# A hybrid decoder layer: the gates of the third and the last recurrent head move behind the last head's levels and scores

## The chip, the cores and the metric

The kernel runs on one core of a Trainium2 chip. The metric is the device time of one execution in microseconds (us). A core has a matrix engine (TensorE, PE in the profile), a vector engine (VectorE, DVE), a scalar engine (ScalarE, ACT), GpSimd (POOL) and a sync engine (SyncE, SP), which issues the transfers here. Each runs its own queue of instructions in order and waits for the others by semaphores.

## The reference

One decoder layer on 2048 tokens of width 1024, in float32. An RMS norm is followed by one projection whose columns feed two groups of heads. Their outputs, side by side, go through an output projection and are added to the input; a gated MLP with a causal depthwise convolution of width 3 and a last RMS norm follow.

The first group has four recurrent heads (HGRN2) of key and value width 128:

```python
f = lb + (1.0 - lb) * jax.nn.sigmoid(hf)
# S_t = diag(f_t) S_{t-1} + k_t v_t^T,  o_t = S_t^T q_t  (k_t = 1 - f_t)
o_hg = hgrn2_chunkwise(q_hg, 1 - f, v_hg, log(f))
o_hg = rmsnorm(o_hg, hg_norm_w) * silu(hg)
```

The last factor is the head's gate: `silu(g) = g * sigmoid(g)`, with g a projection of the normed input. The second group is attention with a window of 128 keys: eight query heads on two key heads, with a learned sink logit in each softmax.

## The kernel before

The sequence is worked in two halves of 1024 tokens, one after the other. In each half the loop of the stage called "mix" runs over h = 0 to 3. Step h holds one recurrent head and one pair of attention heads (attention j = h). After the four steps come the output projection (`out_proj`), the gate and up projections of the MLP (`gate_up`) and the down projection (`down`). Texts count the heads from 1: the third head is h = 2, the last is h = 3.

Activations stand with features on the 128 partitions and tokens along the free axis. To keep float32 accuracy with fast matmuls, an operand is split in two parts, hi and lo (`split`, lines 208 and 209, and for weights `prep`, lines 178 and 179: a cast on ACT and a subtraction on DVE), and three products are added. A projection, `unit` (line 197), is 8 x 3 x 2 = 48 matmuls of 128x512 into two PSUM banks. The banks come in three sets: "mm" with four, "hg" and "at" with two each.

A recurrent head (`hgrn`) is a Python generator that hands back control at its `yield`s:

- f and q: two projections ("f" and "hq" in the profile), a sigmoid, and q into one of eight slots named "hg".
- levels: K = 1 - f and Q = q f (line 433; both have one buffer), the diagonal products (`pdiag`, line 441), then for m = 1, 2, 4, 8, 16, 32, 64 a set of products `plev` (lines 467 and 480) between neighbouring blocks of m tokens, each followed on DVE by an update of K and Q (lines 473, 474, 483, 484) and by a masked copy into ST. The next level's products need the updated K (gathered by ACT into G, line 465) and Q. F, the running product of f, starts as the f tile itself.
- state: K is transposed (`pkn`), the chunk updates `pu` are formed, and a chain of eight DVE steps makes the states SS.
- gate: the projection g (`gate`), its product with the norm factors `invb` (line 450, into q's tile, since q has been used up), sigmoid (line 451), product (line 452).
- output: 16 products `po` (lines 531 and 532), squares on ACT (line 533), an inverse root on DVE, scaling to `on`, transposes `pot` back (line 545), and the product of `pot`, the norm weight and the gate (line 546) into mix[h].

For the last head, the gate comes before the levels, and mix[3] is split at once (lines 550 and 551).

Attention (`attend`) has four parts: the projection of q ("q", slot "att"), scores with softmax (`psc`, then `sc`, lines 343 to 383), and for each group of 512 tokens the transposes `ppt` and products with V (`poT`). `project_v` makes the recurrent values for two heads at a time, at h = 0 and h = 2.

`out_proj` needs mix[0] to mix[7] in split form. The split tiles take the places of the half's input X, which become free only when the last projection of the stage has read them. Each of its units goes over the eight inputs in the order 0, 4, 1, 5, 2, 6, 7, 3, so a unit can begin before mix[7] and mix[3] exist. Its second unit may start only behind the last head's level m = 8, its third only behind `po` (`AFTER`).

The order in which each engine gets its instructions isn't the program's order alone. The program is handed to a scheduler, which plays it through with its own model of durations: among the instructions that could go, the one that stands earlier in the program goes first. So an early place is a priority, and a projection that stands late can still be taken as filling where nothing earlier is ready. Tiles of one tag share a fixed number of buffers: "f" (the f tile, the gate's sigmoid) has two, K, Q and SS one.

The loop over the heads calls the generators by `next`:

```python
next(hg); next(hg); next(at)        # f and q, levels, attention q
# values at even h, weights of the gate
next(at); next(hg); next(hg)        # scores, state, gate
next(at); next(at); next(hg)        # two groups of V products, output
```

Step 3 goes in another order: f and q, attention q, gate, six splits, levels, scores, state, first group of V, output, second group.

Of the kernel before, what the change touches and what calls it, by code (L numbers as in the profile page):

```python
# [8 lines left out]
F32 = mybir.dt.float32  # L9
# [3 lines left out]
AF = mybir.ActivationFunctionType  # L13
ALU = mybir.AluOpType
# [3 lines left out]
P = 128  # L18
# [3 lines left out]
HALF = 1024  # L22
# [3 lines left out]
HG = 4  # L26
# [19 lines left out]
def hymba_layer(ctx: ExitStack, tc: tile.TileContext, a: dict, out: bass.AP):  # L46
    nc = tc.nc
# [22 lines left out]
    def halves():  # L70
        return [(b, slice(b * 512, (b + 1) * 512)) for b in range(NB)]
# [132 lines left out]
    def split(src, w=None, eng=None, dst=None):  # L204

        h, l = dst or new_x()
        if w is None:
            nc.scalar.copy(h, src)
            (eng or nc.vector).tensor_tensor(l, src, h.bitcast(F32), op=ALU.subtract)  # L209
        else:  # L210
            nc.scalar.activation(h, src, AF.Identity, scale=w)
            nc.vector.scalar_tensor_tensor(l, src, w, h.bitcast(F32), op0=ALU.mult, op1=ALU.subtract)
        return h, l
# [68 lines left out]
    def blocks(t, turn=False):  # L282

        v = t.rearrange("p (g r) -> p g r", r=32)
        return v[:, :, ::-1] if turn else v
# [131 lines left out]
    def hgrn(hf, h, X, invb, vs, WG, mix, p, fu=None):  # L417

        fu = fu or unit(a["w_f"][h], X, "f")
        f = p.tile([P, HALF], F32, tag="f", name="f", bufs=2)  # L420
# [4 lines left out]
        q = slot(f"hg{h}")  # L425
# [17 lines left out]
                                    ident.unsqueeze(1).to_broadcast([P, 4, P]), op=ALU.mult)  # L443


        def gate():
            gu = unit(WG.get(h, a["w_g"][h]), X, "g")
            s = p.tile([P, HALF], F32, tag="f", name="sg", bufs=2)
            for b, bs in halves():
                nc.vector.tensor_tensor(blocks(q[:, bs], b), blocks(gu[b]), blocks(invb[:, bs]), op=ALU.mult)  # L450
                nc.scalar.activation(s[:, bs], q[:, bs], AF.Sigmoid)
                nc.vector.tensor_tensor(q[:, bs], q[:, bs], s[:, bs], op=ALU.mult)

        if h == HG - 1:
            gate()
            yield
        F = f
        for m in LEVELS:
            nb = HALF // (2 * m)
# [35 lines left out]
            for s0 in range(0, P, 2 * m):  # L495
                nc.scalar.copy(ST[s0:s0 + m, :, s0 + m:s0 + 2 * m],
                               pl[s0:s0 + m, 0:TT * m].rearrange("p (c m) -> p c m", c=TT))
        yield
        v = vs[h]

        Kn = p.tile([P, TT, P], F32, tag="t4", name="Kn", bufs=2)
# [7 lines left out]
        for b in range(NB):  # L509
# [4 lines left out]
            for i in range(4):  # L514
# [3 lines left out]
                                               op0=ALU.mult, op1=ALU.add)  # L518
        yield
        g = q  # L520
        if h < HG - 1:
            gate()
            yield
        on = p.tile([P, TT, P], F32, tag="t4", name="on", bufs=2)
# [9 lines left out]
        rs = rsqrt(ss, TT, 1.0 / P)  # L534
# [7 lines left out]
        for b, bs in halves():  # L542
            pt = ps("hg", "pot")
            for i in range(4):
                nc.tensor.transpose(pt[:, i * P:(i + 1) * P], on[:, 4 * b + i], ident)
            nc.vector.scalar_tensor_tensor(blocks(g[:, bs]), blocks(pt, b), C.hgw, blocks(g[:, bs]),
                                           op0=ALU.mult, op1=ALU.mult)
            if h == HG - 1:
                hi, lo = mix[h]
                nc.scalar.copy(hi[:, bs], g[:, bs])  # L550
                nc.vector.tensor_tensor(lo[:, bs], g[:, bs], hi[:, bs].bitcast(F32), op=ALU.subtract)
        nc.vector.tensor_copy(state[:, h], SS[:, TT - 1])
        yield

    def project_v(hf, pr, X, rs, p):

# [416 lines left out]
    X, W = [], []  # L973
# [5 lines left out]
    f0 = unit(a["w_f"][0], X, "f", kind="aux", then={4: xs.spread})  # L979
    nxt = X, kv, xs.acc, xs.rs, f0  # L980
    for hf in range(NH):
        X, kv, invb, rs, f0 = nxt
        with ExitStack() as st:
            p = pool(f"mix{hf}", stack=st, reuse_waits="tile")
            KS, V = att_keys(hf, kv, invb, p)
            mix = [None] * KT
            vs = []
            M, WG = {}, {}
            for h in range(HG):
                hg = hgrn(hf, h, X, invb, vs, WG, mix, p, f0 if h == 0 else None)  # L990
                at = attend(hf, h, X, invb, KS, V, mix, p)
                next(hg)
                if h == HG - 1:
                    next(at)
                    next(hg)
                    for kt in (0, 4, 1, 5, 2, 6):
                        M[kt] = split(mix[kt])
                    next(hg)
                else:
                    next(hg)  # L1000
                    next(at)
                if h % 2 == 0:
                    vs += project_v(hf, h // 2, X, rs, p)
                if h < HG - 1:
                    WG[h] = prep(a["w_g"][h])
                next(at)
                next(hg)
                if h < HG - 1:
                    next(hg)
                next(at)  # L1010
                if h < HG - 1:
                    next(at)
                    next(hg)
                else:
                    next(hg)
                    next(at)
            M[7], M[3] = mix[7], mix[3]
        with ExitStack() as st:
            p = pool(f"ffn{hf}", stack=st, reuse_waits="tile")
            kept, ops, hs, first = out_proj(hf, M, p)  # L1020
            acts = gate_up(hf, ops, hs, first, p)
            nxt = down(hf, kept, acts, p)
# [62 lines left out]
```

## Time and profile before

| what | us |
|---|---|
| time before, median of 3 runs | 2219.83 (2214.84 to 2221.45) |
| the profiled execution's own time | 2216.09 |
| its span, first to last instruction | 2214.4 |
| PE busy | 2173.3 |
| DVE busy | 1637.8 |
| ACT busy | 1047.8 |
| first matmul of the output projection, first half | 336.3 |
| first matmul of gate_up, first half | 462.8 |
| first matmul of down, first half | 880.7 |

A profile comes from one execution. Lines such as L197 are lines of the kernel, `out<-in` names the tile written and the tiles read. A float32 matmul of two unsplit operands is listed as two matmuls. Matmuls are pipelined, so their listed durations overlap.

### The profile page before, as it was taken

Reading aid. Unit: us, or ns where it says so; the run is one execution under the profiler, and the core shown is the slowest. Engines: PE = TensorE matmul, PEld = TensorE weight load, DVE = VectorE, ACT = ScalarE, POOL = GpSimd, SP = SyncE. Lnnn points to the kernel's source line nnn. Section 1 sums busy time; section 2 is a strip of 40 time slices with the busy share of each in tenths; the row PEclk is TensorE's granted clock in tenths of the full one; section 3 lists DMA queues with packets and bytes.
Section 4 is the critical chain, followed back from the end, with each engine's and each line's share of the span. In section 5 each row is a group of like instructions: output and inputs, shape, how many; then the busy total and the mean of one; then the engine's idle time right before and its main releaser. Section 6 shows DMA issues by size and latency. Waiting matters only on the chain.

```text
span 2214.4 us, 29214 instructions
## 1 busy us (share of the span) xinstructions
PE 2173.3 (98%) x11302; PEld 1818.8 (82%) x11302; DVE 1637.8 (74%) x2458; ACT 1047.8 (47%) x1821; POOL 13.0 (1%) x37
## 2 busy tenths in 40 slices
PE   8999998999999999999999999989999999999997
PEld 6988987778888888888889889878788888888887
DVE  6567568688887888775865666577878888887766
ACT  6445445454444445335725455545544444443353
POOL 2000000000000000000000000000000000000000
PEclk9999999999999999999999999999999999999998
DMA  4111112322333234964631111213232323359643
GB/s 154 39 29 39 29 39 67 107 84 92 113 100 114 88 127 146 372 233 160 201 124 39 29 29 39 67 29 132 66 126 85 124 87 119 96 196 388 223 130 128
DMA packets 89995, 254.15 MB, mean 115 GB/s; under 512 B 11008, under 2 KB 13184, under 8 KB 89856
## 3 DMA queue, kind: packets, MB, share of 16 engines
q1 hardware_dynamic: 87552, 251.17, 33.8%
q8 instruction: 88, 1.44, 0.3%
q10 hardware_dynamic: 2304, 1.12, 0.2%
q14 instruction: 51, 0.42, 0.1%
HBM read 195.10 MB, written 57.15 MB: 114 GB/s over the span
## 4 chain that ended last, share of the span: by engine, by line
PE 94%; DVE 3%; ACT 1%; DMA 1%; issue 0%; SPq 0%; DVEq 0%; ACTq 0%
PE X L697 7%; PE X L698 7%; PE X L699 7%; PE pop L197 6%; PE hq L197 4%; PE f L197 4%; PE q L197 4%; PE g L197 4%; PE pdx L879 4%; PE pdx L880 4%; PE pdx L881 4%; PE Y L697 4%; PE Y L699 4%; PE Y L698 4%; PE pdy L880 3%; PE pdy L879 3%
## 5 line engine op out<-in xcount | busy, mean ns | idle before, releaser
L574 ACT CAST whi<-raw 128x1024 fp32r<-128x1024 f32 x88 | 92.7, 1053 | 109.3 <-PE X L698 66.8
L698 PE MATMUL X<-T,whi 128*128 128x512 f32 x352 | 137.3, 390 | 0.0
L697 PE MATMUL X<-T,whi 128*128 128x512 f32 x352 | 137.0, 389 | 0.0
L699 PE MATMUL X<-T,wlo 128*128 128x512 f32 x352 | 136.9, 389 | 0.0
L763 DVE SCALAR_TENSOR_TENSOR y<-ga,cw,y 128x1024 f32<-128x1024 f32 x88 | 112.5, 1279 | 28.1 <-ACT y L761 28.1
L703 ACT COPY u<-X 128x512 f32<-128x512 f32 x88 | 51.6, 587 | 121.6 <-PE X L699 121.3
L575 DVE TENSOR_TENSOR wlo<-raw,whi 128x1024 fp32r<-128x1024 f32 x88 | 107.2, 1218 | 0.0
L575 DVE TENSOR_TENSOR xld<-raw,xhd 128x1024 fp32r<-128x1024 f32 x72 | 80.8, 1132 | 18.9 <-ACT xhd L574 18.6
L178 ACT CAST whi<-raw 128x1024 fp32r<-128x1024 f32 (+2 forms) x61 | 63.0, 1035 | 62.0 <-PE hq L197 12.4
L574 ACT CAST xhd<-raw 128x1024 fp32r<-128x1024 f32 x72 | 69.6, 978 | 43.2 <-DMA raw<-act0T 14.7
L197 PE MATMUL pop<-XL,whi 128*128 128x512 f32 x256 | 84.8, 395 | 3.5 <-DVE XL L209 3.5
L197 PE MATMUL pop<-XH,wlo 128*128 128x512 f32 x256 | 83.8, 393 | 0.8 <-DVE wlo L179 0.8
L197 PE MATMUL pop<-XH,whi 128*128 128x512 f32 x256 | 84.1, 400 | 0.2
L179 DVE TENSOR_TENSOR wlo<-raw,whi 128x1024 fp32r<-128x1024 f32 (+2 forms) x61 | 73.2, 1204 | 13.2 <-ACT whi L178 13.2
L697 PEld LDWEIGHTS X<-T,whi 128*128 128x128 f32 x352 | 66.1, 188 | 14.0 <-ACT u L703 0.3
L699 PEld LDWEIGHTS X<-T,wlo 128*128 128x128 f32 x352 | 66.1, 188 | 13.9 <-issue 0.2
L698 PEld LDWEIGHTS X<-T,whi 128*128 128x128 f32 x352 | 66.1, 188 | 13.9 <-issue 0.2
L879 PE MATMUL pdx<-xhd,hid 128*128 128x512 f32 x192 | 74.5, 391 | 1.0 <-ACT hid L574 1.0
L880 PE MATMUL pdx<-xld,hid 128*128 128x512 f32 x192 | 74.8, 390 | 0.0
L697 PE MATMUL X<-T,Sh 128*128 128x512 f32 x176 | 68.7, 390 | 5.3 <-ACT s L703 5.3
L881 PE MATMUL pdx<-xhd,lod 128*128 128x512 f32 x192 | 73.7, 389 | 0.0
L567 PE MATMUL pvv<-whi,XL 128*128 128x256 f32 x256 | 73.1, 287 | 0.0
(359 smaller groups left out, 6530.8 us busy)
## 6 DMA issues: line engine op xcount, KB each, us to landing
wr<-in_w_down SPq DMA_DIRECT2D x90, 512.0 KB, 5.6
raw<-in_w_gate SPq DMA_DIRECT2D x44, 512.0 KB, 3.7
raw<-in_w_up SPq DMA_DIRECT2D x44, 512.0 KB, 3.6
raw<-act0T SPq DMA_DIRECT2D x20, 512.0 KB, 5.9
raw<-act1T SPq DMA_DIRECT2D x20, 512.0 KB, 5.6
act0B<-y SPq DMA_DIRECT2D x33, 256.0 KB, 2.3
act1B<-y SPq DMA_DIRECT2D x33, 256.0 KB, 2.5
raw<-in_w_out SPq DMA_DIRECT2D x16, 512.0 KB, 4.0
```

What stands on the lines that cost most here:

```text
L179: nc.vector.tensor_tensor(lo[:, c], raw[:, c], hi[:, c].bitcast(F32), op=ALU.subtract)
L197: nc.tensor.matmul(o[b], w, x[:, bs], start=f, stop=l)
L567: nc.tensor.matmul(o[:, 0:256], xl[:, t], hi[:, c], start=False, stop=False)
L574: nc.scalar.copy(h, src)
L575: (eng or nc.vector).tensor_tensor(l, src, h.bitcast(F32), op=ALU.subtract)
L697: nc.tensor.matmul(o, wh[:, ws], xh, start=i == 0 and not more, stop=False, skip_group_check=more)
L698: nc.tensor.matmul(o, wh[:, ws], xl, start=False, stop=False, skip_group_check=more)
L699: nc.tensor.matmul(o, wl[:, ws], xh, start=False, stop=i == 3, skip_group_check=more)
L763: nc.vector.scalar_tensor_tensor(y, g[:, w:w + HALF], C.cw[:, ft, w:w + 1], y, op0=ALU.mult, op1=ALU.add)
L879: nc.tensor.matmul(o, wh[:, i, c], ah[:, i, cols], start=f, stop=False, skip_group_check=more)
L880: nc.tensor.matmul(o, wh[:, i, c], al[:, i, cols], start=False, stop=False, skip_group_check=more)
L881: nc.tensor.matmul(o, wl[:, i, c], ah[:, i, cols], start=False, stop=l, skip_group_check=more)
```

## The change

The loop handles heads 1 and 2 as before. Heads 3 and 4 are written out with the generators of both open at once:

- third head: f and q, levels, attention q, values, scores, state; then f and q of the last head; then the third head's first group of V, its output without the gate, its second group of V;
- last head: attention q, levels, scores;
- the gate of the third head, the gate of the last head, the six splits;
- the last head's state, first group of V, output, second group of V.

For the third head (`late`) the output is evicted from PSUM by ACT with the norm weight as scale into q's tile. Its gate, which comes later, puts g times `invb` in a tile of its own ("ug", tag "f"), and has one product more: q by ug, then q by the sigmoid. The third head's gate weights are no longer loaded ahead at an explicit place but inside its projection.

```diff
+        late = h == HG - 2
+
         def gate():
             gu = unit(WG.get(h, a["w_g"][h]), X, "g")
             s = p.tile([P, HALF], F32, tag="f", name="sg", bufs=2)
+            t = p.tile([P, HALF], F32, tag="f", name="ug", bufs=2) if late else q
             for b, bs in halves():
-                nc.vector.tensor_tensor(blocks(q[:, bs], b), blocks(gu[b]), blocks(invb[:, bs]), op=ALU.mult)
-                nc.scalar.activation(s[:, bs], q[:, bs], AF.Sigmoid)
+                nc.vector.tensor_tensor(blocks(t[:, bs], b), blocks(gu[b]), blocks(invb[:, bs]), op=ALU.mult)
+                nc.scalar.activation(s[:, bs], t[:, bs], AF.Sigmoid)
+                if late:
+                    nc.vector.tensor_tensor(q[:, bs], q[:, bs], t[:, bs], op=ALU.mult)
                 nc.vector.tensor_tensor(q[:, bs], q[:, bs], s[:, bs], op=ALU.mult)
 
-        if h == HG - 1:
-            gate()
-            yield
         F = f
         for m in LEVELS:
...
         yield
+        if h == HG - 1:
+            gate()
+            yield
         v = vs[h]
...
         g = q
-        if h < HG - 1:
+        if h < HG - 2:
             gate()
             yield
...
-            nc.vector.scalar_tensor_tensor(blocks(g[:, bs]), blocks(pt, b), C.hgw, blocks(g[:, bs]),
-                                           op0=ALU.mult, op1=ALU.mult)
+            if late:
+                nc.scalar.activation(blocks(q[:, bs]), blocks(pt, b), AF.Identity, scale=C.hgw)
+            else:
+                nc.vector.scalar_tensor_tensor(blocks(g[:, bs]), blocks(pt, b), C.hgw, blocks(g[:, bs]),
+                                               op0=ALU.mult, op1=ALU.mult)
...
         yield
+        if late:
+            gate()
+            yield
...
+            for h in range(HG - 2):
+                hg, at = head(h)
+                step(hg, hg, at)
                 if h % 2 == 0:
                     vs += project_v(hf, h // 2, X, rs, p)
+                WG[h] = prep(a["w_g"][h])
+                step(at, hg, hg, at, at, hg)
+            (h2, a2), (h3, a3) = head(HG - 2), head(HG - 1)
+            step(h2, h2, a2)
+            vs += project_v(hf, 1, X, rs, p)
+            step(a2, h2, h3, a2, h2, a2)
+            step(a3, h3, a3, h2, h3)
+            for kt in (0, 4, 1, 5, 2, 6):
+                M[kt] = split(mix[kt])
+            step(h3, a3, h3, a3)
             M[7], M[3] = mix[7], mix[3]
```

Here `head(h)` makes the two generators of a head, and `step(...)` calls `next` on each of its arguments in turn. The lines of the old loop that these replace are left out.

More of the change, by code (lines that the diff above doesn't have):

```diff
@@ L988, in hymba_layer, with head, step @@
             M, WG = {}, {}
[L989 to L1001, printed above, removed]
+            def head(h):
+                return (hgrn(hf, h, X, invb, vs, WG, mix, p, f0 if h == 0 else None),
+                        attend(hf, h, X, invb, KS, V, mix, p))
+            def step(*gens):
+                for g in gens:
+                    next(g)
+            for h in range(HG - 2):
+                hg, at = head(h)
+                step(hg, hg, at)
                 if h % 2 == 0:
                     vs += project_v(hf, h // 2, X, rs, p)
[L1004 to L1016, printed above, removed]
+                WG[h] = prep(a["w_g"][h])
[8 more added lines that the diff above has]
+            step(h3, a3, h3, a3)
             M[7], M[3] = mix[7], mix[3]
```

## The prediction, on record before the result

> **What bounds the kernel now.** I read the page first: the busy time of the engines and the shares of the chain that ended last.
>
> ```profile
> PE 2173.3 (98%) x11302; PEld 1818.8 (82%) x11302; DVE 1637.8 (74%) x2458; ACT 1047.8 (47%) x1821; POOL 13.0 (1%) x37
> PE 94%; DVE 3%; ACT 1%; DMA 1%; issue 0%; SPq 0%; DVEq 0%; ACTq 0%
> ```
>
> TensorE (PE) sets the end. The change adds and removes no matmul, so all it can win or lose is PE's idle time (2214.4 - 2173.3 = 41 us) and time at a lowered clock. Next, the busy time by stretches around the last heads of both sequence halves. The columns are length, then busy us of PE, its weight loads, VectorE (DVE), ScalarE (ACT) and GpSimd, then the granted clock and DMA.
>
> ```profile
> 310.00:325.00 15.00, 15.00 (x101) 12.73 (x100) 1.93 (x4) 3.28 (x12) 0.00 (x0) 1.00 0.13 37
> 325.00:345.00 20.00, 20.00 (x105) 17.04 (x104) 17.82 (x33) 14.94 (x26) 0.00 (x0) 1.00 0.42 132
> 345.00:365.00 20.00, 14.39 (x78) 11.91 (x77) 19.39 (x34) 11.82 (x30) 0.00 (x0) 0.86 0.26 79
> 365.00:385.00 20.00, 20.00 (x189) 16.83 (x188) 13.79 (x24) 7.83 (x29) 0.00 (x0) 0.97 0.01 2
> 1405.00:1420.00 15.00, 15.00 (x96) 12.42 (x95) 2.42 (x3) 2.96 (x10) 0.00 (x0) 1.00 0.10 36
> 1440.00:1460.00 20.00, 14.42 (x91) 11.98 (x90) 19.78 (x33) 13.70 (x35) 0.00 (x0) 1.00 0.27 79
> ```
>
> This is the picture of the case: for 15 us DVE has almost nothing to do (1.93 and 2.42 us), and 20 to 25 us later it is full (19.39 and 19.78 of 20) while PE starves (14.39 and 14.42 of 20). The waits of PE in the two tails (300 to 420 us, then 1400 to 1540 us) name the sufferers:
>
> ```profile
> PE plev L467 <- ACT G L465: 1.9, 1, 1.9
> PE pop L197 <- DVE XL L209: 1.8, 1, 1.8
> PE plev L467 <- DVE Q L474: 1.4, 2, 1.2
> PE po L531 <- ACT on L533: 1.0, 2, 0.5
> PE psc L356 <- DVE sc L365: 0.4, 1, 0.4
> ...
> PE plev L467 <- DVE Q L474: 3.2, 2, 2.0
> PE pop L197 <- DVE XL L209: 1.7, 1, 1.7
> PE po L531 <- ACT on L533: 1.0, 2, 0.5
> PE poT L403 <- DVE pp L395: 0.9, 2, 0.7
> PE psc L356 <- DVE sc L365: 0.4, 1, 0.4
> ```
>
> They are the last head's levels (plev), the output projection (pop) waiting for its split inputs (XL), and scores. Without the po line they sum to 1.9 + 1.8 + 1.4 + 0.4 = 5.5 us in the first half and 3.2 + 1.7 + 0.9 + 0.4 = 6.2 us in the second: 11.7 us in all that the change can reach. The po line (2 x 1.0) is the ping-pong of PE and ACT on the output chunks, which the change leaves alone. The first half shows one more loss, in the clock column:
>
> ```profile
> 355.00:360.00 5.00, 2.39 (x16) 1.82 (x15) 5.00 (x12) 2.89 (x6) 0.00 (x0) 0.94 0.17 66
> 360.00:365.00 5.00, 4.32 (x14) 3.85 (x15) 4.46 (x10) 3.21 (x14) 0.00 (x0) 0.50 0.00 0
> 365.00:370.00 5.00, 5.00 (x21) 4.04 (x20) 2.91 (x7) 4.27 (x22) 0.00 (x0) 0.88 0.02 3
> ```
>
> Right after the worst stretch (2.39 of 5 busy) PE ran at half clock. The loss is (0.06 + 0.50 + 0.12) x 5 = 3.4 us. The second half has stalls as large and no such dip.
>
> **The change, part by part.** Four rows show where the DVE hole comes from, as the engines' lines in order of time and the chain have them:
>
> ```profile
> 324.92 1.23 DVE L433 TENSOR_TENSOR Q<-hg,f 128x1024 f32<-128x1024 f32 x1 [13.07 <-PE po L532]
> 325.35 10.89 PE g L197 x48
> 336.47 3.66 PE pop L197 x16
> 346.56 1.12 PE L467 MATMUL plev<-Q,G 128*128 128x128 f32 x8
> ```
>
> The last head's Q has one buffer and waits 13.07 us for the third head's output products (po). Meanwhile PE runs projections. A projection of 48 matmuls costs PE 10.89 us. Before the change PE takes them in the order: gate of head 3, f, q (hq), attention q of head 4, gate of head 4, then out-projection. The unit of attention q ends only at 325, so the last scores (which need it) fall into 336 to 370, where DVE is full with levels and splits.
>
> (1) *Head 3's gate leaves its place.* PE stays full there, as f, hq and q move up by one unit each: cost nothing, the cover is the same 32.7 us of projections (three units of 10.89). If that cover were gone, the price would be up to 10.89 us per half. With it attention q ends near 325 - 10.9 = 314 us. Its scores can start about 11 us sooner, in the hole.
>
> (2) *What the scores are worth to DVE.* The groups of head 3 and 4 by shape (count, busy us, mean ns of one):
>
> ```profile
> L365 DVE COPY_PREDICATED sc<-own,psc 128x256 f32<-128x256 uint32 x16 | 7.0, 447 | 1.2 <-ACT sc L362 0.6 <-ACT sc L364 0.6
> L383 DVE TENSOR_TENSOR sc<-sc,den 128x1024 f32<-128x1024 f32 x4 | 4.9, 1223 | 0.1
> L368 DVE TENSOR_REDUCE m<-sc 128x8 f32<-128x1024 f32 x4 | 4.9, 1215 | 0.1
> L345 DVE TENSOR_TENSOR ql<-att,qh 64x512 fp32r<-64x512 f32 x6 | 4.1, 684 | 0.6 <-ACT qh L343 0.4
> L450 DVE TENSOR_TENSOR hg<-g,invb 128x512 f32<-128x512 f32 x4 | 2.7, 684 | 2.1 <-PE g L197 2.1
> L452 DVE TENSOR_TENSOR hg<-hg,sg 128x512 f32<-128x512 f32 x4 | 2.6, 680 | 0.0
> L546 DVE SCALAR_TENSOR_TENSOR hg<-pot,hgw,hg 128x512 f32<-128x512 f32 x4 | 2.8, 747 | 4.9 <-PE pot L545 4.9
> ...
> L407 ACT COPY att<-poT 128x512 f32<-128x512 f32 x2 | 1.2, 586 | 5.1 <-PE poT L403 5.1
> ```
>
> One head's scores take 8 x 0.447 + 2 x 1.223 + 2 x 1.215 + 4 x 0.684 = 11.2 us of DVE. Between nothing and all of that fits the 15 us hole; I take half, 5.6 us, since each score step also goes through PE and ACT and a quarter of the hole is over when the scores begin. ACT has the same hole (3.28 of 15).
>
> (3) *Head 3's gate joins the tail*: two products with invb, two with its own sigmoid (4 x 0.68) and the two new q x t products of the same shape, 6 x 0.68 = 4.1 us on DVE; its two products L546 (2 x 0.75 = 1.5) become ScalarE evictions, for which the trace has no row; the nearest, the PSUM copy L407, says 0.59 us, and the DVE form 0.75 is the upper end: I take 0.6 each, hidden in ACT (11.82 of 20 busy). The q x t product waits for that eviction; what stands behind it on DVE (level products, splits) would wait up to those 0.6 us too, and PE's plev and pop for them. Net on DVE in the tail: 4.1 - 1.5 = 2.6 us more.
>
> (4) *Head 4's gate and the six splits step behind its levels and scores.* DVE does the same work, but a level's product no longer queues behind a 1.2 us split. The cost on PE is nothing while out-projection or a gate's 10.89 us is there to be run.
>
> (5) *Transfers.* The three projections' weights (and w_g of head 3, now loaded inside its unit) come through the same SyncE queue, the same three raw buffers and the same hi/lo pair, only in another order; none of PE's waits above names a transfer or a weight. I take nothing; if one came late by its ACT and DVE conversion, PE would lose about 1 us (the DVE half of such a conversion has a 128x1024 shape, like the 1.22 us of L383).
>
> **The sum.** DVE sheds 5.6 and takes 2.6 in the tail, so it is 3 us lighter per half, and (4) puts what is left into a better order. PE lacked 5.6 us in each full stretch. I take two thirds of the reachable 11.7 us, 7.8 us; the bounds are nothing (the stalls only move) and all of it. The half clock followed a stretch half empty; with the stalls cut I take 3.0 of its 3.4 us, bounds 0 and 3.4. On the profiled execution, 2216.09 us (span 2214.4 and 1.7 around it): 2216.1 - 7.8 - 3.0 = 2205.3. That execution lies 3.7 below the median 2219.83; the runs spread from 2214.84 to 2221.45, which dips of 3.4 us that come in some executions and not in others would give (an estimate from the one dip seen). I put 1.7 of the 3.7 back: **2207 us**.
>
> [...]
>
> **Rivals.** *The dip stays.* Shorter stalls can still bring the half clock, as two like tails gave one dip: only 7.8 is won on the clean part, 2216.1 - 7.8 + 1.7 = 2210. [...]
>
> *Only the order of the fillers changes.* PE is full until 345 us in both versions and runs the same five projections by then; levels still wait for Q, which still waits for po. Then the last head's chain starts when it did and the stalls stay: 2216 to 2220, say 2217. For it speaks the 13.07 us wait, which no edit shortens; against it the DVE hole beside the full stretch.
>
> *PSUM banks held by the late gates: slower.* The projections share four "mm" banks. Head 3's gate sum leaves its two banks only through a new tile "ug", which shares two "f" buffers with head 4's f (alive until its first level) and the sigmoid; head 4's gate sum leaves only when q has been read by the diagonal products, just before plev at 346.6. If both wait, out-projection, which now starts at 336.5, cannot start before some 347 to 350 us, and PE loses the 16 + 8 + 8 matmuls (32 x 10.89/48 = 7.3 us) with which it bridged to 352. Twice 7.3, less half the stalls (5.8): 2216.1 + 14.6 - 5.8 = 2225. It decides from the point where the banks are held 3.9 us (7.8/2) per half beyond 336.5. Against it: ug's first product may take the free f buffer at once.
>
> *All of it goes*: 2216.1 - 11.7 - 3.4 - 1.0 = 2200, if half of the po waits find cover too.
>
> **How the numbers follow.** What a measurement of this kernel can tell from no change is 0.3%, 6.7 us: faster is below 2213. Chances: forecast 2207 0.35, dip stays 2210 0.10, all gone 2200 0.12, only the order 2217 0.29, banks held 2225 0.14. Faster 0.35 + 0.10 + 0.12 = 0.57, same 0.29, slower 0.14. The likeliest case's own range is 2203 to 2211. For 8 in 10 the range takes in the unchanged case and half of the all-gone case and stops short of held banks: 2200 to 2221.
>
> **What will show it.** Right: DVE busy well above 2 us in the 15 us before the last Q; the last psc matmuls before or early in the levels; PE idle in each tail at 2 to 4 us instead of 7 to 8; clock 1.00 throughout; out-projection's end, and with it everything after, 4 us sooner in each half. Wrong: the first half's levels starting at 346 us as now with the same waits on Q and G (only the order), or a gap of several us on PE before the first pop with the gates' sums unread (banks held), or waits of g and hq on whi or wlo (transfers).

## The result, and the profile after

The changed kernel takes 2216.83 us in the median (2213.91 to 2219.96) against 2220.1 us before (2214.84 to 2222.14), 20 executions each. The ratio is 0.9987, with a 95% interval of 0.9981 to 0.9993: a gain of 3.3 us, or 0.13%, which is real by its interval but less than the 0.3% that the prediction called "no change". The forecast was 2207 us. The time stands beside the rival "only the order of the fillers changes" (2217). One execution of the whole study was out of line with its kernel (4800.05 us, with the changed kernel's splits on GpSimd); no median or ratio here moves with it.

The profiled execution took 2213.91 us, its span 2212.2. First the page's line of engine busy time.

```profile
PE 2175.0 (98%) x11302; PEld 1822.3 (82%) x11302; DVE 1638.0 (74%) x2458; ACT 1049.3 (47%) x1825; POOL 14.4 (1%) x37
```

DVE has the same count and busy time as before (1637.8). The four ScalarE instructions more are the evictions that replace DVE's. Next, the busy time in the stretches of both tails; the columns are length, then busy us of PE, its weight loads, DVE, ACT and GpSimd, then the granted clock and DMA.

```profile
310.00:325.00 15.00, 15.00 (x99) 12.44 (x98) 6.43 (x13) 9.75 (x23) 0.00 (x0) 1.00 0.13 37
325.00:345.00 20.00, 20.00 (x109) 17.20 (x108) 19.37 (x37) 13.61 (x24) 0.00 (x0) 1.00 0.43 132
345.00:365.00 20.00, 15.50 (x102) 13.13 (x101) 18.93 (x31) 12.31 (x29) 0.00 (x0) 0.91 0.18 54
365.00:385.00 20.00, 19.04 (x162) 16.02 (x161) 10.29 (x19) 6.36 (x23) 0.00 (x0) 1.00 0.08 26
1405.00:1420.00 15.00, 15.00 (x96) 12.12 (x96) 7.15 (x21) 8.79 (x23) 0.00 (x0) 1.00 0.13 36
1440.00:1460.00 20.00, 17.51 (x110) 14.52 (x109) 18.88 (x31) 13.18 (x34) 0.00 (x0) 0.91 0.27 80
```

The hole did fill, by 6.43 - 1.93 = 4.5 us in the first half and 7.15 - 2.42 = 4.7 in the second. But the stretch in which the last head's levels run, 345 to 365, is nearly as full as it was: 18.93 instead of 19.39. What DVE gained in the hole it lost behind that stretch, from 365 to 385, where it had been busy for 13.79 us and now is for 10.29; there PE had been busy for all 20 us. Over all 75 us from 310 to 385 DVE's work went from 52.9 to 55.0 us.

PE's waits in the first tail (300 to 420 us) and in the second (1400 to 1540 us), in us in total, count and longest:

```profile
PE poT L403 <- DVE pp L395: 3.4, 2, 3.1
PE plev L469 <- DVE Q L476: 1.0, 1, 1.0
PE po L536 <- ACT on L538: 1.0, 2, 0.5
PE plev L482 <- DVE K L486: 0.7, 1, 0.7
...
PE ppt L392 <- DVE sc L365: 0.2, 1, 0.2
...
PE poT L403 <- DVE pp L395: 2.3, 1, 2.3
PE po L536 <- ACT on L538: 1.0, 2, 0.5
PE po L536 <- DVE SS L522: 0.7, 1, 0.7
...
PE pu L518 <- ACT Kn L512: 0.2, 1, 0.2
PE pop L197 <- ACT XH L208: 0.2, 1, 0.2
```

The waits of out-projection on split inputs (1.8 and 1.7) and of the levels on G (1.9) are gone. A new one has come: attention's output transposes (poT) wait for the masked copies of the probabilities (pp), 3.1 and 2.3 us at a stretch. Counted as the prediction counted them (without po's wait on ACT, and without a wait of 0.4 us on a weight that each tail had before and has now), the waits are 3.4 + 1.0 + 0.7 + 0.2 = 5.3 us in the first half and 2.3 + 0.7 + 0.2 + 0.2 = 3.4 in the second, 8.7 instead of 11.7. That is 3.0 us less, close to the 3.3 us by which the time fell. The clock gave nothing: the first half lost 3.4 us to it before, and now each half loses 0.09 x 20 = 1.8, and as much again goes in a dip at 1563.7, where the kernel before has none.

Why the levels' stretch stayed full is seen on DVE's own line, in order of time (start us, us, operation), between the Q update that the products of level m = 4 need and the one that those of m = 8 need:

```profile
353.00 0.68 DVE L476 TENSOR_TENSOR Q<-Q,F 128x512 f32<-128x512 f32 x1
353.60 1.31 DVE L493 COPY_PREDICATED ST<-lmask,plev 128x512 f32<-128x512 uint32 x1
354.70 0.73 DVE L457 TENSOR_TENSOR hg<-hg,sg 128x512 f32<-128x512 f32 x1
355.35 1.20 DVE L368 TENSOR_REDUCE m<-sc 128x8 f32<-128x1024 f32 x1
356.47 0.68 DVE L395 TENSOR_TENSOR po<-ppt,ownT 128x512 f32<-128x512 f32 x1
357.07 0.68 DVE L457 TENSOR_TENSOR hg<-hg,sg 128x512 f32<-128x512 f32 x1
357.67 0.68 DVE L395 TENSOR_TENSOR pp<-ppt,prevT 128x512 f32<-128x512 f32 x1
358.27 0.68 DVE L395 TENSOR_TENSOR po<-ppt,ownT 128x512 f32<-128x512 f32 x1
358.87 0.68 DVE L395 TENSOR_TENSOR pp<-ppt,prevT 128x512 f32<-128x512 f32 x1
359.46 0.68 DVE L475 TENSOR_TENSOR K<-K,F 128x512 f32<-128x512 f32 x1
360.06 1.21 DVE L209 TENSOR_TENSOR XL<-hg,XH 128x1024 fp32r<-128x1024 f32 x1
361.20 0.68 DVE L476 TENSOR_TENSOR Q<-Q,F 128x512 f32<-128x512 f32 x1
```

From 354.70 to 359.46 DVE does 4.8 us of work that no level needs (gate products L457, the max of the scores L368, masked copies L395), then between K and Q a split of 1.1 us. All the while PE's next level product waits, and for 3.1 us of it PE is idle, until the masked copies let poT begin. The two gate products in these rows are the last head's. The third head's are these, with the sigmoids on ACT:

```profile
337.01 1.28 DVE L456 TENSOR_TENSOR hg<-hg,ug 128x512 f32<-128x512 f32 x2
350.04 1.15 ACT L454 ACTIVATE sg<-ug 128x512 f32<-128x512 f32 x2
351.80 1.28 DVE L457 TENSOR_TENSOR hg<-hg,sg 128x512 f32<-128x512 f32 x2
```

Four of the third gate's six products (those with `invb`, from 327.41, and with ug) are done before the levels begin. Its sigmoids come late, after exponentials of the last head's scores and a load of ACT's function table (ACT_TABLE_LOAD, 1.28 us, at 348.75), and its last two products fall among the levels. Only behind them can the third head's output be split, at 360.06. PE's line shows the result; here the products (plev) of m = 4 and m = 8 and the transposes behind the last level (pkn):

```profile
346.05 1.07 PE L469 MATMUL plev<-Q,G 128*128 128x128 f32 x8
...
353.74 1.16 PE L469 MATMUL plev<-Q,G 128*128 128x128 f32 x8 [1.02 <-DVE Q L476]
363.67 1.05 PE L469 MATMUL plev<-Q,G 128*128 128x128 f32 x8
...
381.98 1.09 PE L511 MATMUL pkn<-ident,K 128*128 128x128 f32 x8
```

From the first plev to pkn the chain takes 381.98 - 346.05 = 35.9 us. Before, it was this:

```profile
346.56 1.12 PE L467 MATMUL plev<-Q,G 128*128 128x128 f32 x8
...
380.78 1.04 PE L506 MATMUL pkn<-ident,K 128*128 128x128 f32 x8
```

That is 34.2 us. So the chain starts when it did and is no shorter, although Q stands 3 us sooner and the diagonal products (pdiag) 6.5 us sooner (337.84 instead of 344.31).

### The profile page after: what moved, and what is told of

Read it like the earlier page. It is cut to its first block, busy times and chain, and to the rows that moved or that the text cites. A ratio compares the mean times of both kernels' runs of the same rounds, so it can differ in the third digit from the quotient of the medians.

```text
span 2212.2 us, 29221 instructions
## 1 busy us (share of the span) xinstructions
PE 2175.0 (98%) x11302; PEld 1822.3 (82%) x11302; DVE 1638.0 (74%) x2458; ACT 1049.3 (47%) x1825; POOL 14.4 (1%) x37
## 4 chain that ended last, share of the span: by engine, by line
PE 95%; DVE 3%; ACT 1%; DMA 1%; issue 0%; ACTq 0%; DVEq 0%
PE X L708 7%; PE X L709 7%; PE X L710 7%; PE pop L197 6%; PE q L197 4%; PE hq L197 4%; PE f L197 4%; PE pdx L890 4%; PE pdx L891 4%; PE Y L708 4%; PE pdx L892 4%; PE Y L710 4%; PE Y L709 4%; PE g L197 4%; PE pdy L891 3%; PE pdy L890 3%
```

## The experiments

The question is where the expected gain went. The texts on record weigh theories against each other by letter: D says that the amount of DVE work in the full stretch sets the stall; O that the order of the work does, or that only the fillers' order changed; V, later, that the masked copies of attention's values (L395) are let into the levels too early; G, also later, that the third gate's own work among the levels does the harm. Each run is compared with runs of the kernel before on the same chip; ratios are to that kernel. Three edits are in the change: the last head's f and q come early, the last gate and the splits come late, and the third gate comes late. The experiments undo or do them alone.

**Splits on GpSimd, after and before.** The six split subtractions leave DVE.

```diff
-                M[kt] = split(mix[kt])
+                M[kt] = split(mix[kt], eng=nc.gpsimd)
```

> The changed kernel with the subtractions of the six split inputs of the output projection (6 x 1.22 us per half) on GpSimd instead of VectorE. Theory D (VectorE is full from 325 to 365 us, and the last head's level updates queue behind other work there): 7.3 us per half leave VectorE, the 10 us gap between the levels m = 4 and m = 8 shrinks to 5 to 6 us, PE's idle time in the two tails (now 6.9 and 4.9 us) falls by half, time about 2211. Rival O (PE waits because of the order in which instructions were laid in the queues, whatever VectorE's load): VectorE only gets idle time, PE's idle time stays at 10 us or more, time 2215 to 2219. If a GpSimd subtraction takes several us, PE waits on the split inputs (XL) instead and the time goes above 2220.

> The kernel before with the same six subtractions per half on GpSimd. Theory D: PE's idle time in the tails (7.0 and 7.7 us) falls by half, and so does the half-rate stretch that follows it: 2210 to 2214. Rival O: 2218 to 2222.

Measured: 2221.14 us, ratio 1.0007 (0.9998 to 1.0016), for the first, 2227.28 us, ratio 1.0033 (1.0020 to 1.0045), for the second. It decides nothing between the theories, since moving the work brought a cost of its own. Two lines of the first in order of time, then two groups of it between 325 and 365 us by shape (count, busy us, mean ns):

```profile
329.53 3.14 POOL L209 TENSOR_TENSOR XL<-hg,XH 128x1024 fp32r<-128x1024 f32 x1 [316.94 <-ACT XH L208]
330.81 2.41 DVE L345 TENSOR_TENSOR ql<-att,qh 64x512 fp32r<-64x512 f32 x1
...
L456 DVE TENSOR_TENSOR hg<-hg,ug 128x512 f32<-128x512 f32 x2 | 3.5, 1771 | 0.0
L457 DVE TENSOR_TENSOR hg<-hg,sg 128x512 f32<-128x512 f32 x4 | 2.6, 681 | 0.0
```

While GpSimd subtracts, a DVE product beside it takes 2.41 us instead of 0.68, and L456 takes 1771 ns in the mean; the same group took 682 ns in the changed kernel. L457 kept its 681, though two of its four ran beside the first us of a subtraction (at 354.43), which then took 4.00 us. So DVE got less relief than the list of moved instructions says.

**The third gate back in its place.** Early f and q and the late last gate stay; the third head's gate goes back between its state and its output.

```diff
-        late = h == HG - 2
+        late = False
...
-        if h < HG - 2:
+        if h < HG - 1:
             gate()
...
-            step(a2, h2, h3, a2, h2, a2)
-            step(a3, h3, a3, h2, h3)
+            WG[2] = prep(a["w_g"][2])
+            step(a2, h2, h2, h3, a2, h2, a2)
+            step(a3, h3, a3, h3)
```

> The changed kernel with the third head's gate back in its old place (ahead of the last head's f and q, output product on VectorE again); the last head's gate stays behind its levels and scores. Theory D with my step (1): without the third gate's move the last attention q ends near 325 us again, VectorE's hole before the last Q is as empty as before (2 us busy of 15), and the time is that of the kernel before, 2218 to 2221. Rival: the last head's gate alone makes the gain, since its level chain no longer queues behind that gate and the splits: 2216 to 2217.

Measured: 2205.97 us (2203.89 to 2208.47), ratio 0.9941 (0.9928 to 0.9953). This is the fastest kernel of the study: 14 us below the one before and 11 below the changed one (10 by the two ratios). Its windows, its last split, and its chain:

```profile
310.00:325.00 15.00, 15.00 (x99) 12.18 (x99) 6.40 (x16) 4.92 (x16) 0.00 (x0) 1.00 0.02 7
345.00:365.00 20.00, 17.13 (x94) 14.86 (x93) 16.26 (x32) 11.72 (x33) 0.00 (x0) 0.91 0.12 43
365.00:385.00 20.00, 19.22 (x198) 16.61 (x197) 15.36 (x31) 7.68 (x30) 0.00 (x0) 1.00 0.00 1
...
340.31 1.22 DVE L209 TENSOR_TENSOR XL<-att,XH 128x1024 fp32r<-128x1024 f32 x1
...
347.23 1.07 PE L469 MATMUL plev<-Q,G 128*128 128x128 f32 x8
...
353.10 1.05 PE L469 MATMUL plev<-Q,G 128*128 128x128 f32 x8
357.02 2.07 PE L469 MATMUL plev<-Q,G 128*128 128x128 f32 x8 [0.16 <-DVE Q L476]
...
374.64 1.06 PE L511 MATMUL pkn<-ident,K 128*128 128x128 f32 x8
```

The hole is filled as in the changed kernel (6.40 against 6.43). What differs is where the rest lies: 16.26 us on the levels' stretch and 15.36 behind it, where the changed kernel has 18.93 and 10.29. All six splits are done by 341.5, before the levels begin, and m = 8 follows m = 4 after 3.9 us instead of 9.9. The chain starts 1.2 us later than in the changed kernel and takes 27.4 us instead of 35.9. So the move of the third gate alone costs about 11 us, in a change that wins 3. Neither theory foresaw this. The expectation had the hole empty again; it is filled here by the third head's masked copies, Q and the eviction of attention q. And the last head's scores are no help in it: their last products (psc) begin at 356.1, as late as before the change (354.8).

**The other two edits alone.** First the last gate and the splits late and nothing else, as an edit of the kernel before:

```diff
-        if h == HG - 1:
-            gate()
-            yield
         F = f
...
         yield
+        if h == HG - 1:
+            gate()
+            yield
         v = vs[h]
...
+                order = [hg, hg, at] if h < HG - 1 else [hg, at, hg, at, hg]
...
+                for g in [at, hg, hg, at, at, hg] if h < HG - 1 else [hg, at, hg, at]:
+                    next(g)
```

> The kernel before with one edit: the last head's gate and the six splits behind its levels and scores; the third head and the place of the last f and q as before. If the last gate's and the splits' place alone makes the gain of the run with the third gate back: 2205 to 2208. If the early f and q are needed too (po of the third head and the last Q came 3 to 6 us earlier there): 2211 to 2216.

Measured: 2220.6 us, ratio 0.9998 (0.9990 to 1.0007): nothing, and outside both expectations. The levels' stretch has 19.49 us of DVE, and the chain takes 33.1 us. But on the engines the edit moved almost nothing: the last two splits stand at 349.2 and 352.1 (before: 349.1 and 352.0), the gate's products with the sigmoid at 354.7 and 356.2 (before: 354.6 and 355.5). So the run shows what this edit of the program does, and not what a really later place of that work would do.

Then f and q early and nothing else, as an edit of the kernel with the third gate back:

```diff
+        if h == HG - 1:
+            gate()
+            yield
         F = f
...
-            step(a3, h3, a3, h3)
+            step(a3, h3)
             for kt in (0, 4, 1, 5, 2, 6):
                 M[kt] = split(mix[kt])
-            step(h3, a3, h3, a3)
+            step(h3, a3, h3, a3, h3, a3)
```

> Only the early f and q of the last head: third gate as before the change, last gate and splits ahead of the last levels as before the change. Theory D (VectorE's load among the levels sets the time): the early f and q bring forward VectorE work and the last attention q, but the last gate (4 x 0.68 us) and the six splits stand among the levels again, so a part is lost: 2209 to 2214, VectorE 17 to 18 of 20 us busy in the full stretch. If the early f and q are all of the gain of the run with the third gate back: 2205 to 2208.

Measured: 2208.95 us, ratio 0.9954 (0.9941 to 0.9966). The chain takes 25.9 us, with 16.66 us of DVE in the levels' stretch. The splits, which the expectation had among the levels again, are done before them here too. So the early f and q alone win 11 of the 14 us. The late last gate adds some 3 us to it or nothing; the two intervals overlap.

**The third gate ahead of the levels.** The late form of the gate stays, but it stands between the last head's attention q and its levels, on the changed kernel:

```diff
-            step(a3, h3, a3, h2, h3)
+            step(a3, h2, h3, a3, h3)
```

> The changed kernel with the third head's gate, in its late form (product on ScalarE, one more product on VectorE), between the last attention q and the last head's levels instead of behind the scores. Theory G: the third gate's VectorE work now stands ahead of the levels and no longer among them, the chain from first level to pkn is 27 to 30 us: 2206 to 2211. Theory V: the scores and V products are as early as in the changed kernel, 2214 to 2218.

Measured: 2208.85 us, ratio 0.9948 (0.9936 to 0.9961). The same arithmetic (six products, two evictions on ScalarE), ahead of the chain in program order, costs some 3 us against its old place or nothing (the intervals overlap), where behind the chain in program order it costs 11. So it is not the late form of the gate that costs, but the place in the program.

The way in which theory G expected this did not come, though. The chain takes 37.5 us in the first half and 32.6 in the second, not 27 to 30. On the engines the gate's last two products still stand among the levels (347.79 and 348.40, first level at 343.32), and so do the last two splits (360.34 and 363.02). In the first half ACT loads its function table four times from 345.83 to 353.56, 1.28 us each, as sigmoids and exponentials alternate; a gate product at the head of DVE's queue waits for that, and the levels wait behind it:

```profile
351.77 1.29 DVE L457 TENSOR_TENSOR hg<-hg,sg 128x512 f32<-128x512 f32 x2 [2.69 <-ACT sg L454]
```

PE waits 5.8 us for Q in this tail, with DVE busy for only 15.01 of the 20 us. The gain lies in the second half, where PE is idle for 2.1 us from 1440 to 1500 (changed kernel 4.5). What does stand elsewhere than in the changed kernel are the first masked copies of V: at 367.5 instead of 356.5, and at 1462.3 instead of 1449.5.

**The third gate's arithmetic left out.** The sigmoid and the gate products of the third head are left out of the changed kernel (its projection and the product with `invb` stay), so this kernel does not gate that head.

```diff
                 nc.vector.tensor_tensor(blocks(t[:, bs], b), blocks(gu[b]), blocks(invb[:, bs]), op=ALU.mult)
+                if late:
+                    continue
                 nc.scalar.activation(s[:, bs], t[:, bs], AF.Sigmoid)
-                if late:
-                    nc.vector.tensor_tensor(q[:, bs], q[:, bs], t[:, bs], op=ALU.mult)
```

> The changed kernel without the third head's gate arithmetic: its projection and the eviction by invb stay, the sigmoid and the four products of each half on VectorE (q by ug, q by the sigmoid, 2.7 us per half) are left out, so the third head's output has no gate. Theory G: that work is what stands among the levels: 2207 to 2211. Theory V: 2214 to 2217.

Measured: 2210.71 us, ratio 0.9960 (0.9947 to 0.9972). Four products of 0.68 us per half are gone, 5.4 us in all, and the time is 6.1 us below the changed kernel's. But the two sums are not the same work: two of the four products had stood ahead of the levels, and the last two splits (2 x 1.2 us), the first of which needs the gated output, are now done before the levels (338.5 and 342.3 in the first half). So the run fits theory G in a wider sense: the gate's work, and what stands behind it, was among the levels.

**The masked copies of V behind the level m = 16.** On the changed kernel, DVE may begin them only behind the Q update of that level:

```diff
+                with tc.issue_after(marks["dve", 16].ins) if j == ATT_J - 1 else ExitStack():
                     for dst, mk in zip(pm[kv], (C.ownT, C.prevT)):
                         nc.vector.tensor_tensor(dst, ptv, mk.unsqueeze(1).to_broadcast([P, 4, P]), op=ALU.mult)
```

> The changed kernel with the masked copies of the last attention head's V products on VectorE (16 x 0.68 us in all, 8 per half; they keep their place otherwise) put behind the last recurrent head's Q update of level m = 16. Theory V (the earlier scores let the V products' copies onto VectorE between the level updates m = 4 and m = 8, and that is what stretches the chain from the first level to pkn to 36 us against 27 us with the third gate back): the gap m = 4 to m = 8 falls from 10 us to about 7, the new wait of poT on pp goes or moves behind m = 16, time 2209 to 2213. Theory G (the third gate's own work does it): 2215 to 2218, the gap stays.

Measured: 2213.83 us, ratio 0.9967 (0.9956 to 0.9978), 3 us below the changed kernel and between the two theories' ranges. The longest wait of its first tail:

```profile
PE pop L197 <- DVE XL L209: 3.6, 1, 3.6
```

The wait of poT is gone, and out-projection waits for a split instead. The stall moved; only part of it was won.

A cruder way, the last head's first group of V put behind its output in program order (`step(h3, h3, a3, a3)` in place of `step(h3, a3, h3, a3)`), made it worse.

> The changed kernel with the last attention head's first group of V products behind the last recurrent head's output instead of ahead of it. Rival O: the new waits of PE on the masked copies (poT on pp, 3.1 and 2.3 us) stand ahead of the levels m = 8 and vanish, the levels from m = 8 on come 3 us sooner, time 2212 to 2214. Theory D: VectorE has the same work in the same stretch; the wait moves to the levels or to the end, where mix[7] is now later: 2216 to 2220.

Measured: 2230.79 us, ratio 1.0053 (1.0041 to 1.0066), above both expectations. The waits on pp stayed, 3.1 and 2.3 us, and each half got a new one of the output's transposes (pot) on DVE (on), 3.6 us. Putting V last in the program left it where it was among the levels.

The delayed masked copies were also tried on the two better orders, the third gate back and the third gate ahead.

> The run with the third gate back, with the masked copies of the last V products behind the Q update of level m = 16 besides. There these copies already come at 370 us, behind m = 32: theory D expects the same time within 2 us of 2206; a gain of more than 3 us would say that they still stood in the way.

> The run with the third gate ahead of the levels in its late form, with the masked copies of the last V products behind m = 16. Theory V: its scores are early, so the copies still stand among the levels; behind m = 16 the chain shortens in the first half, 2204 to 2207. Theory G alone: 2208 to 2210.

Measured: 2206.59 us, ratio 0.9943 (0.9929 to 0.9957), and 2212.02 us, ratio 0.9962 (0.9949 to 0.9974). Neither is better than without the delay (2205.97 and 2208.85), and the second lies above both of its ranges. With the third gate back, the masked copies come only at 370.75 anyway, so nothing was expected there. With the third gate ahead, a gain was expected and none came, but the trace shows that there was little to delay: of the first four copies of each half, two stand ahead of the Q update of m = 16 in the first half (367.5 and 368.2, the update at 370.05) and none in the second. So neither run tests theory V; the only one that does is the one on the changed kernel.

**DVE work added among the levels.** To the kernel with the third gate back, four products of 0.68 us were added per half, behind the Q update of m = 2 of the last head, on a tile that nobody reads.

```diff
+            if h == HG - 1 and m == 2:
+                with tc.issue_after(upd.ins):
+                    for _ in range(4):
+                        nc.vector.tensor_tensor(extra, ident.unsqueeze(1).to_broadcast([P, 4, P]), C.own.unsqueeze(1).to_broadcast([P, 4, P]), op=ALU.mult)
```

> The run with the third gate back, plus four VectorE products of 128x512 per half on a tile nobody reads (4 x 0.68 = 2.7 us, as much as the third gate's two times two late products), put behind the Q update of the last head's level m = 2. A price: theory D expects 2 x 2.7 us of delay in the chain, of which PE loses at least half, 2209 to 2212. If VectorE's load among the levels doesn't matter: 2205 to 2207.

Measured: 2211.79 us, ratio 0.9962 (0.9950 to 0.9975). Added were 2 x 2.7 = 5.4 us; the time rose by 5.8 us, or by 0.0021 x 2220 = 4.7 when each kernel is compared on its own chip. The intervals of the two ratios touch, but the single runs don't (2203.89 to 2208.47 against 2210.32 to 2213.52). Its window and chain:

```profile
345.00:365.00 20.00, 15.92 (x89) 13.64 (x87) 19.01 (x36) 9.35 (x21) 0.00 (x0) 0.91 0.20 71
...
347.77 1.07 PE L470 MATMUL plev<-Q,G 128*128 128x128 f32 x8
...
379.96 1.03 PE L516 MATMUL pkn<-ident,K 128*128 128x128 f32 x8
```

DVE is as full as in the changed kernel, and the chain is 32.2 us long instead of 27.4. In this run one us of foreign work on DVE among these levels costs about one us of the kernel; with intervals that touch, the price is not known more closely.

## Why the prediction was wrong, point by point

**What bounds the kernel** was read rightly as far as it went: PE is busy for 98%, the waits in the two tails are what can be won, and the gain of 3.3 us answers to 3.0 us fewer waits. What was not read is that the level waits belong to one chain, plev, DVE's Q update, plev, through seven levels. The 20 us of full DVE were taken as a load; they are a chain with other work in it.

**(1) The third gate leaves its place at no cost.** This held where the gate left: PE stayed full from 310 to 345, and attention q ended at 310.6 (forecast 314). But the cost of a move lies also where the step goes, and undoing this one edit won 11 us. A second value was put at nothing here without a reason, the early f and q ("move up by one unit each: cost nothing"): alone they win 11 us.

**(2) Scores into the hole, 5.6 us:** the hole took 4.5 and 4.7 us more, near the forecast by luck. Only 2.2 us in the first half and 1.8 in the second are work of the scores (three and two of L345, one L365); most of the rest of the growth is Q (1.2 us) and the inverse root, which came sooner because po did. And early scores are not what pays: the two fastest kernels, both with the third gate back, have them as late as before (psc from 356.1 and 357.8, against 354.8).

**(3) The third gate joins the tail, 2.6 us net on DVE: the step that failed.** It was right as a sum: DVE's work from 310 to 385 grew by 2.1 us, and the evictions on ScalarE, taken at 0.6 us, take 682 ns each (group L552). As a price it was wrong. The 2.6 was set against the 5.6 as if all DVE time in the tail were alike, which made the move of the third gate a relief of 3 us per half; the runs show a loss of about 11 us in all. The relief came mostly out of 365 to 385 (13.79 to 10.29), where PE had been busy throughout. Among the levels stand now two of the gate's products, the last head's two behind them, the split that waits for the gate and the one behind that, and four masked copies. With the third gate back, all of these come in the first half before the levels or behind m = 32. And the one run that only adds work there loses about a us for a us.

**(4) "Puts what is left into a better order", at no cost:** wrong. A level's product did stop queueing behind the two splits that stood at 349.09 and 351.95. It queues now behind gate products, a max, masked copies and two splits at 360.06 and 362.40. Alone the edit gives 0.9998, and on the engines it hardly moves an instruction.

**(5) Transfers at nothing:** right. No new wait names a weight. The prediction's reading that none of the waits names one missed a small wait of out-projection on wlo, 0.4 us in each tail, the same before and after.

**The sum:** two thirds of 11.7 us were taken, 3.0 came. Of the 3.0 us for the clock nothing came, since a dip of half the length now stands in each half: the rival "the dip stays" was right on that.

**The rivals.** "Only the order of the fillers changes" named the time (2217) and one sign to look for, the first half's levels starting at 346 as before; they start at 346.05. The other sign, the same waits on Q and G, did not come (G's is gone), and in the second half the levels start at 1438.5 instead of 1442.6. Its reason does not hold either: it said that Q waits for po and that no edit shortens that. The wait went from 13.07 to 3.50 us, and Q stood at 322.02 instead of 324.92. The equal time is two large effects that cancel, early f and q by -11 and the third gate by about +11, with the late last gate at 0 to -3. "PSUM banks held by the late gates" did not come about: ug is read out of its bank at 327.41, and PE was full until out-projection began at 342.96.

**What stays open.** Why early f and q shorten the chain from 34 to 26 us is read from the traces, not tested by itself. In both kernels that have them without the late third gate, the splits are done before the levels and the masked copies come after m = 32. The program's planner lays that order, and no run forced it by itself. Of the 11 us that the third gate costs, the left-out arithmetic gives 6.1, the delayed copies 3.0 and the gate ahead of the levels 8.0; these overlap, and how much is due to the gate's own products, to the splits behind them, to the masked copies or to ACT's table loads was not separated. Why the delayed copies cost about 3 us (intervals overlapping) with the third gate ahead is not known either.

No one figure orders the kernels. The table has, for the first and second half, DVE's busy time in the 20 us from 345 and from 1440, the length of the chain from the first level to pkn, and PE's idle time from 345 to 400 and from 1440 to 1500. DVE's load and the chain's length fail in places (the chain is longest with the third gate ahead, a fast kernel), since PE may have other work while a level waits. PE's idle time goes with the time best. These are single executions, and the times are medians.

| kernel | DVE busy, us | chain, us | PE idle, us | time us |
|---|---|---|---|---|
| both groups of V behind the output | 18.76 / 19.95 | 34.7 / 34.9 | 12.5 / 10.2 | 2230.8 |
| last gate late alone | 19.49 / 19.78 | 33.1 / 36.5 | 6.6 / 7.8 | 2220.6 |
| before | 19.39 / 19.78 | 34.2 / 33.6 | 6.6 / 7.5 | 2220 |
| changed | 18.93 / 18.88 | 35.9 / 36.5 | 6.4 / 4.5 | 2216.8 |
| masked copies behind m = 16 | 17.31 / 17.98 | 34.7 / 33.4 | 5.8 / 3.4 | 2213.8 |
| third gate ahead, copies behind m = 16 | 15.03 / 17.29 | 37.3 / 32.6 | 6.8 / 2.1 | 2212.0 |
| third gate back, products added | 19.01 / 18.02 | 32.2 / 28.8 | 6.5 / 4.8 | 2211.8 |
| third gate's arithmetic out | 17.43 / 17.53 | 33.8 / 37.6 | 4.0 / 4.3 | 2210.7 |
| f and q early alone | 16.66 / 16.16 | 25.9 / 27.3 | 3.5 / 5.9 | 2209.0 |
| third gate ahead | 15.01 / 17.44 | 37.5 / 32.6 | 5.9 / 2.1 | 2208.9 |
| third gate back, copies behind m = 16 | 17.77 / 16.62 | 25.9 / 26.3 | 3.7 / 3.9 | 2206.6 |
| third gate back | 16.26 / 16.63 | 27.4 / 26.3 | 3.7 / 3.8 | 2206.0 |

## What to carry to other kernels

Before costing a moved step, find the dependent chain that will run around its new place, and price each instruction on that chain's engine at its full length as a first estimate, even where the busiest engine has other work to run; the same gate cost 11 us behind the levels in program order and little ahead of them. Count what comes behind the moved step as well, here two splits. Read in the trace where a moved step really ran: of the edits here, one left the engines' order almost as it was, and two put work among the levels that stands ahead of them or behind them in the program. A sum of an engine's work over a stretch says nothing on where in it the relief falls. And a compound change that moves the time little is worth taking apart: here, one of three edits ate what another had won.

## What was not expected of the hardware

**Half clock came in equal pieces of 3.4 us, and also where no wait was as long as that.** One stretch at half clock of the kernel with the third gate ahead, then stretches of 3.41 us that end where a half-clock stretch begins or could begin, two of the kernel before and one of the changed one:

```profile
353.69:363.93 10.24, 7.75 (x26) 6.64 (x27) 8.29 (x13) 6.63 (x22) 0.00 (x0) 0.50 0.12 30
...
355.99:359.40 3.41, 1.53 (x12) 1.16 (x10) 3.41 (x9) 2.31 (x4) 0.00 (x0) 1.00 0.02 10
1455.07:1458.48 3.41, 1.66 (x11) 1.57 (x12) 3.41 (x8) 3.05 (x15) 0.00 (x0) 1.00 0.00 0
...
1447.62:1451.03 3.41, 1.07 (x9) 0.91 (x10) 3.41 (x5) 0.57 (x1) 0.00 (x0) 1.00 0.00 0
```

Here 10.24 / 2 = 5.1 us are lost. The kernel before lost 3.4 (6.8 at half rate), the changed one 1.7 in each tail (3.4 at half rate). These are three, two and one pieces of 3.4 us. The longest wait of PE in the first tail of the kernel before was 1.9 us, and of the changed one 3.1, both shorter than a piece; in the kernel before PE was busy for 1.53 of the 3.41 us ahead of its dip.

How empty PE's time was ahead of half clock, the traces show roughly. In each trace the half-clock stretches begin whole steps of 3.413 us apart (1092.27 us, or 320.0 steps, between those of the changed kernel's two tails). Lay the 14 traces out in these steps, from 20 us to the half-clock stretch at each kernel's end. Then every step at full clock with PE busy for up to 1.54 us is followed by half clock, 42 in all, and of those with 1.58 us or more only two are (1.64 and 1.77, both with the third gate's arithmetic left out). At the kernels' ends half clock follows steps of 1.15 to 1.99 us. So in these traces the limit lies near half a step (1.54 to 1.58 of 3.41 us), and is not sharp in these busy times. It also tells the two like tails of the kernel before apart: the first had 1.53 us in its emptiest step and dipped, the second 1.66 us and did not.

**DVE products took longer beside GpSimd.** In the changed kernel with its splits on GpSimd, the subtraction takes 3.14 us (2.4 to 4.0 over the six) where DVE's takes 1.21, and DVE products beside it take up to 2.41 us for 0.68. Not every product did (L457 kept its 681 ns), and why some did was not shown.
